# An encoder block on one core: query loads a unit earlier, gate stores on another queue, weight blocks a product later

## The chip, the cores and the metric

The kernel runs on one core of a Trainium2 chip. The metric is the device time of one execution in microseconds, as the median of several. The core's engines are TensorE (PE, with its weight loads shown as PEld), VectorE (DVE), ScalarE (ACT), GpSimd (POOL) and SyncE (SP). Each runs its own instruction stream in order. SP, ACT and POOL also issue DMA transfers; such an issue stands in the stream of its engine, behind what was written before it.

## The reference

One encoder layer over 1024 tokens of width 1024, all in float32:

```python
h = h + 0.5 * swiglu(rms_norm(h, ffn1_norm), ...)
u = rms_norm(h, mix_norm)
z = u @ w_in
q, k, v, s_in, gates = jnp.split(z, splits, axis=-1)
y_attn = neighbourhood_attention(q, k, v, na_rpb) @ w_attn_out
y_ssm = s5_branch(s_in, ...) @ w_ssm_out
g_attn, g_ssm = jnp.split(jax.nn.sigmoid(gates), 2, axis=-1)
h = h + (g_attn * y_attn + g_ssm * y_ssm) @ w_out
h = h + 0.5 * swiglu(rms_norm(h, ffn2_norm), ...)
h = h + (p @ w_ple_proj) * sigmoid(rms_norm(h, ple_norm) @ w_ple_gate)
return rms_norm(h, final_norm)
```

The attention has 8 heads of 64 over a grid of 16 rows by 64 columns, with a window of 8 by 16 and a learned bias per head. The state-space branch is a scan in both directions. The gates are two blocks of 1024 columns of `z`.

## The kernel before

Activations are kept transposed (features on the 128 partitions, tokens along the free axis, in two halves of 512). Each float32 operand is split into a high part, rounded to the type that TensorE takes (`split`, a cast on ACT at L159), and the rest (a subtraction on DVE at L160); a product of 128x128 by 128x512 is then three matmuls (`mm3`, L190 to L192). Large products use a recursive scheme with seven products for a two by two block product, in the order of `A7`, `ACC7` and `NEW7`.

The stages run in this order: first feed-forward block; the mixer; merging of the branches and output projection; second feed-forward block; the per-layer embedding; the final norm. The change is in the mixer alone.

In the mixer two streams of work are interleaved by hand on PE. The **main stream** goes through 84 products (`items`, 12 pairs of 7): the query and key projections (`qk`) and the gate projections (`g`). Each product is `s_run`: four `mm3`, and after each of them one `tick()`. A tick moves the **side stream** (`mixer_side`) on; `yield 3` in it means that its next piece comes three ticks later. The side stream does, one after another, the injection into the state-space scan, the attention, the outputs of the scan, and its gated linear unit.

The attention runs over 64 units: head `hd`, half of the rows `rb`, block of columns `cb` (0 to 3). In step `j` of its loop (L1346) the side stream loads the bias table (`load_tab`), asks for queries and keys (`load_q`, L1203; `load_k`, L1197), computes the scores of unit `j` (`attn_scores`, PE at L1228, bias and minimum on DVE at L1232, exponential and scaling on ACT at L1235 and L1237), transposes those of unit `j - 2` (`attn_turn`, PE at L1244), and multiplies unit `j - 4` by the values (`attn_values`, PE at L1255 and L1257). After the last column block of a half the output is put together on ACT and DVE (L1261, L1262) and stored (L1365). Two steps of the scan follow (`scan_steps`, POOL at L1154 to L1156), then `yield 3`. One set of queries, high and low part, serves the four column blocks of a half: `load_q` takes two buffers and issues four DMAs from DRAM through SP (L1208). It can run only when the projections of that head have been stored (`ready`).

The results of a product leave PSUM in `s_evac` (ACT copies at L1539, DVE additions at L1543). Gate results go to `s_out`, which appends their store to the list `later`; the list is emptied by `s_store` (L1546) in the next product, behind its third `mm3`. An entry of `later` names the engine that issues the transfer: ACT for values, keys and queries, POOL for gates (L1518). There are 32 gate stores of 256 KB, into `g_d`, read back after the mixer.

Weight blocks of 128x512 are loaded by `s_load` (L1499) through ACT's queue (L1506) and prepared by `s_prep`. `s_ahead(n + 1)` at the start of product `n` has asked for the loads up to product `n + LL` and the preparations up to `n + LP`, with `LL, LP = 5, 2` (L1567). Of the seven products of a pair, four load a block.

Query, value and weight tiles, the split weights, results on their way out and most other temporaries of the mixer share one pool of 24 buffers of 128x512 (`NM`, tag `m`). A tile that takes over a buffer waits until the last reader of the former one is done, a store included.

PE's order in the mixer is that of the program. The order of the other engines' instructions and DMA issues is set by the planner of the tool, which simulates the kernel with modelled times and picks what is ready by priority; evacuations are given a higher priority.

Of the kernel before, what the change touches and what calls it, by code (L numbers as in the profile page):

```python
# [21 lines left out]
NH = 8  # L22
# [19 lines left out]
def encoder_block(ctx, tc, I, out):  # L42
    nc = tc.nc
# [46 lines left out]
    def bank(name):  # L90
        return ps.tile([P, HT], F32, tag="ps", name=name)

    def dtile(name, shape):
        return dr.tile(list(shape), F32, name=name)
# [28 lines left out]
    g_d = dtile("g_d", [16, P, SEQ])  # L123
# [70 lines left out]
    def hsl(t):  # L194
        return slice(t * HT, (t + 1) * HT)
# [882 lines left out]
    def u_second():  # L1078
        yield 6
        un[1].stat()  # L1080
        yield 1
        for j in (0, 1, 2, 3, 4, 5, 6, 7):
            u_norm(j, 1)
            yield 1
        yield 3
        for k in range(4):
            G.tensor_tensor(h[4 + k][1], h[k][1], h[4 + k][1], ALU.add)
            s3 = tmp("s3")
            G.tensor_tensor(s3, h[k][0], h[k][1], ALU.subtract)
            nc.gpsimd.dma_start(s_d[k], s3)  # L1090
            yield 3
            u_put("s1", h[4 + k][1])
        for k in range(4):
            G.tensor_tensor(h[4 + k][1], h[4 + k][1], h[k][0], ALU.subtract)
            yield 2
            u_put("s2", h[4 + k][1])
        for k in range(4):
            G.tensor_tensor(h[4 + k][0], h[4 + k][0], h[4 + k][1], ALU.subtract)
            yield 2
            u_put("s4", h[4 + k][0])  # L1100
# [6 lines left out]
    def new_x():  # L1107
        xt = tl("h", 1, [P, 2 * XR], F32, "X")
        x0 = xt[:, 0:1]
        X.update(t=x0.tensor, o=x0.offset, p=x0.ap[0], v=xt.rearrange("p (r g n) -> p r g n", r=2, g=NPAIR))  # L1110
        for r in range(2):
            V.memset(X["v"][:, r, :, 0:1], 0.0)
            V.memset(X["v"][:, r, :, XP - 1:XP], 0.0)
# [6 lines left out]
    def inject_load(pr):  # L1120
        fm = [ta("fmi", [P, 256]) for _ in range(2)]
        for d in range(2):
            (nc.sync, nc.scalar)[d].dma_start(fm[d], f_d[pr, :, d * 256:(d + 1) * 256])
        return load_u(pr), fm

    def inject(pr, ut, fm):
        o = bank("inj")
        for g in range(2):
            for d in range(2):
                T.matmul(o[:, (2 * g + d) * NCH:(2 * g + d + 1) * NCH], lhsT=fm[d][:, g * P:(g + 1) * P],  # L1130
                         rhs=ut[:, g], start=True, stop=True)
        for g in range(2):
            for r in range(2):
                dst = X["v"][g * 64:(g + 1) * 64, r, pr, 1:1 + 2 * NCH]
                src = o[r * 64:(r + 1) * 64, g * 256:(g + 1) * 256]
                if g == r:
                    A.copy(dst, src)  # L1137
                else:
                    V.tensor_copy(dst, src)
# [10 lines left out]
    def scan_steps(n):  # L1150
        for c in range(scan["c"], min(scan["c"] + n, NCH)):
            x0, x1 = (xap(o, [[XP, 2 * NPAIR], [257 - 2 * o, 2]]) for o in (c, c + 1))
            both = xap(c, [[0, 2], [XP, 2 * NPAIR], [257 - 2 * c, 2]])
            G.tensor_tensor(sc, both, rho4, ALU.mult)  # L1154
            G.tensor_tensor(cross1, cross1, cross, ALU.add)  # L1155
            G.tensor_tensor(x1, sc[:, 0], x1, ALU.add)  # L1156
            scan["c"] = c + 1
# [52 lines left out]
    def load_v(hd, cb):  # L1210
        n = 4 * KNC[cb]
        hl = tmp("vhl", [P, 4, 2 * 64], F32R)
        nc.sync.dma_start(hl[0:n].rearrange("p g d -> p (g d)").bitcast(F32), vdr[hd, :, KC0[cb]:KC0[cb] + KNC[cb]])
        vld[hd, cb] = hl

    def load_tab(b, v):
        if b < 2 * NH:
            n = 12 * TN[v]
            tabs[b, v] = ta("tb")[:, 0:n]
            nc.sync.dma_start(tabs[b, v], I["tabs"][b, :, TOFF[v]:TOFF[v] + n])  # L1220
# [89 lines left out]
    def mixer_side():  # L1310
        yield from u_second()
        while 3 not in stored:
            yield 1
        yield 7
        new_x()
        ld = {}
        for pr in range(3):
            ld[pr] = inject_load(pr)
        yield 10
        for pr in range(NPAIR):  # L1320
            if pr + 3 < NPAIR:
                ld[pr + 3] = inject_load(pr + 3)
            inject(pr, *ld.pop(pr))
            yield 2
        while "v" not in stored:
            scan_steps(1)
            yield 1
        for cb in range(4):
            scan_steps(4)
            yield 4  # L1330
            load_v(0, cb)
        load_tab(0, 0)
        while 0 not in ready:
            scan_steps(1)
            yield 1
        units = [(hd, rb, cb) for hd in range(NH) for rb in range(2) for cb in range(4)]
        n = len(units)
        load_k(0)
        load_q(0, 0)
        for _ in range(6):  # L1340
            scan_steps(1)
            yield 2
        sms, pts, O = {}, {}, {}
        late.clear()
        lo, so = {}, {}
        for j in range(n + 5):  # L1346
            if j < n:
                hd, rb, cb = units[j]
                b = 2 * hd + rb
                load_tab(b + cb // 2, (1, 2, 0, 0)[cb]) if cb < 3 else None  # L1350
                if cb == 2 and rb == 0:
                    load_q(hd, 1)
                if cb == 2 and rb == 1 and hd + 1 < NH:
                    while hd + 1 not in ready:
                        yield 1
                    load_q(hd + 1, 0)
                if rb == 0 and cb == 2 and hd + 1 in ready:
                    load_k(hd + 1)
                if rb == 1 and cb == 2 and hd + 1 < NH and hd + 1 not in khl:
                    load_k(hd + 1)  # L1360
                sms[j] = attn_scores(hd, rb, cb)
            if 0 <= j - 2 < n:
                pts[j - 2] = attn_turn(units[j - 2][2], sms.pop(j - 2))
            while late:
                nc.scalar.dma_start(*late.pop())  # L1365
            if 0 <= j - 4 < n:
                hd, rb, cb = units[j - 4]
                if cb == 0:
                    O[hd, rb] = bank("O")
                attn_values(hd, rb, cb, O[hd, rb], *pts.pop(j - 4))  # L1370
                if rb == 1 and hd + 1 < NH:
                    load_v(hd + 1, cb)
            scan_steps(2)
            if j >= n:
                if j - n < 3:
                    lo[j - n] = ssm_load(j - n)
            yield 3
        scan_steps(NCH)
        for p in range(NPAIR + 1):
            if 3 <= p + 3 < NPAIR:  # L1380
                lo[p + 3] = ssm_load(p + 3)
            if p < NPAIR:
                so[p] = ssm_out(p, *lo.pop(p))
            if p > 0:
                so.pop(p - 1)()
            yield 1 + p % 2
        yield 3
        glu_load(0)
        raws = [glu_raw(0), glu_raw(1)]
        yield 11  # L1390
        glu_act(0)
        glu_load(1)
        yield 2
        glu_act(1)
        for t in range(2):
            yield from glu_half(t, raws)
# [99 lines left out]
    later = []  # L1496
# [14 lines left out]
    def s_out(n, c, t, second, src):  # L1511
        kind, m = pairs[n]
        if kind == "g":
            if c == "21":
                z, src = tmp("z21"), src
                A.copy(z, src)
                src = z
            later.append((nc.gpsimd, g_d[2 * m + second, :, hsl(t)], src))  # L1518
            return
        hi, lo = tmp("qkh", dt=F32R), tmp("qkl", dt=F32R)  # L1520
        if second:
            A.activation(hi, src, AF.Copy, scale=0.125)
            V.scalar_tensor_tensor(lo, src, 0.125, hi.bitcast(F32), ALU.mult, ALU.subtract)
        else:
            def view(x):
                return x.rearrange("p (b r c) -> p r b c", b=4, r=8)
            sv = src.rearrange("p (r b c) -> p r b c", r=8, b=4)
            A.copy(view(hi), sv)
            V.tensor_tensor(view(lo), sv, view(hi).bitcast(F32), ALU.subtract)
        for i, x in enumerate((hi, lo)):  # L1530
            later.append((nc.scalar, (k_d if second else q_d)[m, i, :, hsl(t)], x.bitcast(F32)))
# [32 lines left out]
        with tc.high_priority(offset=PRI):  # L1564
            s_evac(n, i)

    LL, LP = 5, 2  # L1567
    done_ = {"l": 0, "p": 0}

    def s_ahead(n):  # L1570
# [137 lines left out]
    for m0 in range(0, NK, 2):  # L1708
# [15 lines left out]
        if m0 in (2, 4):  # L1724
            out_load(2 if m0 == 2 else 0)
            with tc.issue_after(mark["gt"]):
                for j in range(NK):
                    t = m0 // 2 - 1
# [229 lines left out]
```

## Time and profile before

| | us |
|---|---|
| median of 3 runs | 2112.91 (2112.85 to 2114.22) |
| the profiled execution | 2113.88 |
| its span, from the first to the last instruction | 2112.1 |
| DVE busy | 1468.4 |
| ACT busy | 1011.0 |
| POOL busy | 480.2 |

The profile page gives the busy time of each engine, the granted clock of TensorE over the span, and the groups of instructions that cost most. Further views of the trace give busy times by stretch, who waited for whom, and the instructions in order of time. In a timeline a row has the start, the duration, engine, line, operation, output and inputs; brackets give the idle time of the engine just before it and what ended that. In a list of waits the numbers are the total, the count and the longest. An engine name with a q (SPq, ACTq) is its DMA queue.

### The profile page before, as it was taken

To read this page: it belongs to the slowest core of one execution; us is meant where nothing else is said; L and a number is where in the kernel's file an instruction comes from. 1 tells how busy PE (TensorE), PEld (TensorE's weight loads), DVE (VectorE), ACT (ScalarE), POOL (GpSimd) and SP (SyncE) were. 2 spreads that over 40 slices of the span, in tenths; PEclk is the share of its full clock that TensorE was granted. 3 is DMA by queue.
4 is the path that set the end of the run, shared out by engine and by line. 5 is a ranking of instruction groups with operands and counts; after the bars stand their busy time and mean duration, and the time that the engine had idled before them with its cause. 6 is when DMAs were issued, how large, how long until landed. Compare 5 with 4: busy or idle time off the path is not lost.

```text
span 2112.1 us, 28243 instructions
## 1 busy us (share of the span) xinstructions
PE 2060.9 (98%) x9518; PEld 1685.9 (80%) x9518; DVE 1468.4 (70%) x2478; ACT 1011.0 (48%) x1878; POOL 480.2 (23%) x720
## 2 busy tenths in 40 slices
PE   9999999999999998898999999999999999999998
PEld 3788888888888887777888788788888888888887
DVE  7897776667967847555655669896565665785855
ACT  6434333344445535656655546553333334445544
POOL 0037565540000518888031002000000000000000
PEclk9999999999999999999999999999999999999999
DMA  3434444485543557566675776143323338533302
GB/s 131 142 118 152 129 131 128 139 284 156 185 120 107 149 180 238 171 197 192 192 243 185 231 264 164 65 154 102 123 80 121 99 100 293 170 105 95 115 26 80
DMA packets 212464, 319.75 MB, mean 151 GB/s; under 512 B 37856, under 2 KB 81504, under 8 KB 212320
## 3 DMA queue, kind: packets, MB, share of 16 engines
q1 hardware_dynamic: 173840, 258.14, 38.9%
q10 hardware_dynamic: 31760, 44.07, 6.3%
q0 software_dynamic: 6720, 15.75, 2.6%
q8 instruction: 75, 1.23, 0.2%
q14 instruction: 69, 0.57, 0.1%
HBM read 224.01 MB, written 93.85 MB: 150 GB/s over the span
## 4 chain that ended last, share of the span: by engine, by line
PE 80%; POOL 7%; DVE 5%; DMA 3%; ACT 2%; issue 2%; SPq 0%; ACTq 0%; DVEq 0%; POOLq 0%
PE dx L190 4%; PE dx L191 4%; PE dx L192 4%; PE gx L190 3%; PE ux L190 3%; PE ux L192 3%; PE gx L192 3%; PE gx L191 3%; PE ux L191 3%; POOL sc L1154 3%; PE dy L192 2%; PE dy L190 2%; PE dy L191 2%; POOL X L1156 2%; POOL sc L1155 2%
## 5 line engine op out<-in xcount | busy, mean ns | idle before, releaser
L159 ACT CAST wh<-hbuf 128x512 fp32r<-128x512 f32 x280 | 173.0, 622 | 389.2 <-PE gx L191 84.3
L160 DVE TENSOR_TENSOR wl<-hbuf,wh 128x512 fp32r<-128x512 f32 x280 | 215.4, 772 | 121.7 <-ACT wh L159 119.7
L159 ACT CAST wh<-wblk 128x512 fp32r<-128x512 f32 x190 | 117.9, 622 | 188.7 <-PE dx L191 82.4
L160 DVE TENSOR_TENSOR wl<-wblk,wh 128x512 fp32r<-128x512 f32 x190 | 130.6, 690 | 49.8 <-ACT wh L159 40.2
L190 PE MATMUL dx<-ah,wh 128*128 128x512 f32 x416 | 163.5, 393 | 0.4 <-DVE hbuf L694 0.3
L192 PE MATMUL dx<-ah,wl 128*128 128x512 f32 x416 | 161.9, 389 | 0.0
L191 PE MATMUL dx<-al,wh 128*128 128x512 f32 x416 | 161.9, 389 | 0.0
L160 DVE TENSOR_TENSOR al<-araw,ah 128x512 fp32r<-128x512 f32 x154 | 106.5, 696 | 49.6 <-PE dx L191 21.1
L190 PE MATMUL gx<-xh,wh 128*128 128x512 f32 x320 | 125.0, 391 | 1.3 <-DVE c L581 1.2
L190 PE MATMUL ux<-xh,wh 128*128 128x512 f32 x320 | 125.0, 390 | 0.0
L191 PE MATMUL gx<-xl,wh 128*128 128x512 f32 x320 | 124.5, 389 | 0.0
L192 PE MATMUL ux<-xh,wl 128*128 128x512 f32 x320 | 124.5, 389 | 0.0
L192 PE MATMUL gx<-xh,wl 128*128 128x512 f32 x320 | 124.5, 389 | 0.0
L191 PE MATMUL ux<-xl,wh 128*128 128x512 f32 x320 | 124.5, 389 | 0.0
L159 ACT CAST ah<-araw 128x512 fp32r<-128x512 f32 x154 | 94.9, 619 | 44.5 <-PE dx L191 14.2
L160 DVE TENSOR_TENSOR wl<-blk,wh 128x512 fp32r<-128x512 f32 x84 | 61.4, 733 | 49.6 <-ACT wh L159 47.2
L190 PEld LDWEIGHTS dx<-ah,wh 128*128 128x128 f32 x416 | 78.1, 188 | 18.6 <-DVE hbuf L694 1.2
L191 PEld LDWEIGHTS dx<-al,wh 128*128 128x128 f32 x416 | 78.1, 188 | 16.8 <-issue 0.7
L428 DVE TENSOR_TENSOR hbuf<-hbuf 128x512 f32<-128x512 f32 x120 | 89.7, 749 | 2.1
L192 PEld LDWEIGHTS dx<-ah,wl 128*128 128x128 f32 x416 | 78.1, 188 | 16.3
L1154 POOL TENSOR_TENSOR sc<-X,rho 128x128 f32<-128x128 f32 x128 | 75.5, 590 | 59.4 <-ACT X L1137 49.6
L190 PE MATMUL px<-xh,wh 128*128 128x512 f32 x192 | 80.6, 420 | 6.1 <-ACT z L1539 4.7
(399 smaller groups left out, 5775.6 us busy)
## 6 DMA issues: line engine op xcount, KB each, us to landing
araw<-a_d SPq DMA_DIRECT2D x154, 256.0 KB
a_d<-c SPq DMA_DIRECT2D x148, 256.0 KB
wblk<-in_wd SPq DMA_DIRECT2D x88, 256.0 KB
hbuf<-in_wg SPq DMA_DIRECT2D x40, 512.0 KB
hbuf<-in_wu SPq DMA_DIRECT2D x40, 512.0 KB
blk<-in_win ACTq DMA_DIRECT2D x48, 256.0 KB
hbuf<-in_xT SPq DMA_DIRECT2D x32, 256.0 KB
h_d<-hbuf ACTq DMA_DIRECT2D x32, 256.0 KB
```

Of the source, the lines that this page charges most:

```text
L159: A.copy(hi, src)
L160: return eng.tensor_tensor(lo, src, hi.bitcast(F32), ALU.subtract)
L190: T.matmul(o, lhsT=wh, rhs=xh, start=first, stop=False, skip_group_check=more)
L191: T.matmul(o, lhsT=wh, rhs=xl, start=False, stop=False, skip_group_check=more)
L192: T.matmul(o, lhsT=wl, rhs=xh, start=False, stop=last, skip_group_check=more)
L428: V.tensor_tensor(b11, (b12, b22, None, None, b21)[i - 2], b11, ALU.subtract)
L1154: G.tensor_tensor(sc, both, rho4, ALU.mult)
L1155: G.tensor_tensor(cross1, cross1, cross, ALU.add)
L1156: G.tensor_tensor(x1, sc[:, 0], x1, ALU.add)
```

## The change

Queries are asked for at column block 1 instead of 2, so three units ahead of their first use instead of two. Gate stores are issued by ACT instead of POOL. Weight blocks are asked for four products ahead instead of five.

```diff
@@ mixer_side
                 load_tab(b + cb // 2, (1, 2, 0, 0)[cb]) if cb < 3 else None
-                if cb == 2 and rb == 0:
+                if cb == 1 and rb == 0:
                     load_q(hd, 1)
-                if cb == 2 and rb == 1 and hd + 1 < NH:
+                if cb == 1 and rb == 1 and hd + 1 < NH:
                     while hd + 1 not in ready:
                         yield 1
                     load_q(hd + 1, 0)
@@ s_out
-            later.append((nc.gpsimd, g_d[2 * m + second, :, hsl(t)], src))
+            later.append((nc.scalar, g_d[2 * m + second, :, hsl(t)], src))
             return
@@
-    LL, LP = 5, 2
+    LL, LP = 4, 2
```

## The prediction

> **What bounds the kernel now.** I read the page's head first, then the busy time by stretches, then the waits of TensorE one by one, and for each long one the timeline of the engine that ended it.
>
> ```profile
> span 2112.1 us, 28243 instructions
> PE 2060.9 (98%) x9518; PEld 1685.9 (80%) x9518; DVE 1468.4 (70%) x2478; ACT 1011.0 (48%) x1878; POOL 480.2 (23%) x720
> 780.00:1065.00 285.00, 257.60 (x1424) 218.24 (x1423) 173.89 (x413) 170.76 (x387) 197.66 (x400) 0.95 0.64 191
> 1065.00:1200.00 135.00, 128.79 (x673) 107.97 (x671) 71.81 (x126) 75.68 (x143) 28.07 (x48) 1.00 0.70 219
> ```
>
> TensorE (PE) is busy 98% of the span, so the change can win only where PE is idle or slow. The last two rows (stretch, its length, busy time of PE, PEld, DVE, ACT, POOL, then the granted clock) cover the mixer's side work. From 780 to 1065, where attention runs, PE is idle 285 - 257.6 = 27.4 us and its clock is 0.95: another 0.05 x 285 = 14 us are lost. From 1065 to 1200 it is idle 6.2 us at full clock. All that the change can win lies in the first row. Its parts, by narrower stretches:
>
> ```profile
> 865.00:885.00 20.00, 14.30 (x71) 11.83 (x70) 8.94 (x24) 9.29 (x22) 17.72 (x37) 0.83 0.40 132
> 955.00:975.00 20.00, 13.96 (x75) 11.78 (x75) 9.77 (x24) 9.99 (x24) 16.94 (x40) 0.83 0.59 182
> 895.00:905.00 10.00, 7.53 (x36) 6.01 (x35) 4.93 (x13) 5.26 (x13) 8.43 (x21) 0.83 0.65 211
> 913.00:930.00 17.00, 14.50 (x78) 12.14 (x77) 8.33 (x21) 10.22 (x24) 14.57 (x32) 0.90 0.75 202
> 985.00:1010.00 25.00, 22.08 (x125) 18.73 (x124) 14.13 (x37) 15.53 (x38) 16.56 (x37) 0.93 0.62 191
> 785.00:805.00 20.00, 16.82 (x68) 13.54 (x67) 11.07 (x19) 9.15 (x20) 17.27 (x35) 0.91 0.69 212
> ```
>
> Each row loses its idle time plus (1 - clock) x length: 5.7 + 3.4 = 9.1; 6.0 + 3.4 = 9.4; 2.5 + 1.7 = 4.2; 2.5 + 1.7 = 4.2; 2.9 + 1.7 = 4.6; 3.2 + 1.8 = 5.0 us. A stall is followed by a stretch at lower clock, so it costs more than its idle time. [...]
>
> The first two losses begin at a gate store:
>
> ```profile
> 859.94 0.69 DVE L1543 TENSOR_TENSOR z<-pz,z 128x512 f32<-128x512 f32 x1 [0.35 <-PE pz L192]
> 868.39 0.58 POOL L1549 DMA_DIRECT2D g_d<-z  x1
> 870.80 0.68 DVE L1262 TENSOR_TENSOR ot<-O,ol 64x512 f32<-64x512 f32 x1 [9.20 <-DMA g_d<-z]
> 872.02 0.54 ACT L1237 ACTIVATE sm<-sm,stat 128x288 f32<-128x288 f32 x1 [9.36 <-DVE stat L1236]
> 872.61 0.87 PE L1244 MATMUL pt<-ident,sm 128*96 128x128 f32 x3 [5.47 <-ACT sm L1237]
> ```
>
> The gate block z is ready at 860.6, but POOL, busy with the scan, issues its store at 868.4. DVE's next output (ot) has been given the buffer of a z, waits 9.2 us for the store to land, and holds everything behind it: ACT's softmax 9.4 us, PE 5.5 us. So some 9.2 - 5.5 = 3.7 us of such a hold are covered.
>
> ```profile
> 945.09 0.59 ACT L1516 COPY z<-px 128x512 f32<-128x512 f32 x1
> 954.12 0.56 POOL L1549 DMA_DIRECT2D g_d<-z  x1
> SPq L1213 <- DMA g_d<-z: 6.8, 1, 6.8
> SPq L1208 <- DMA g_d<-z: 5.8, 1, 5.8
> 965.02 0.58 PE L1228 MATMUL s<-khl,ql 128*128 128x288 f32 x1 [3.35 <-DMA ql<-q_d]
> ```
>
> Here z is ready at 945.7 and stored at 954.1; SP's loads, in one queue, wait for its buffer (6.8, then 5.8 us), and PE waits for the queries. The other three losses are query loads as well:
>
> ```profile
> 983.18 0.34 PE L1228 MATMUL s<-khl,qh 128*128 128x384 f32 x1
> 986.44 0.34 PE L1228 MATMUL s<-khl,qh 128*128 128x384 f32 x1
> 988.05 1.14 SPq L1208 DMA_DIRECT2D qh<-q_d  x2
> 989.28 1.18 SPq L1208 DMA_DIRECT2D ql<-q_d  x2
> 995.39 0.37 PE L1228 MATMUL s<-khl,qh 128*128 128x288 f32 x1 [2.35 <-DMA qh<-q_d]
> 996.33 0.37 PE L1228 MATMUL s<-khl,ql 128*128 128x288 f32 x1 [0.57 <-DMA ql<-q_d]
> 900.61 0.37 PE L1228 MATMUL s<-khl,ql 128*128 128x288 f32 x1 [2.15 <-DMA ql<-q_d]
> 918.10 0.37 PE L1228 MATMUL s<-khl,ql 128*128 128x288 f32 x1 [0.61 <-DMA ql<-q_d]
> 1025.29 0.37 PE L1228 MATMUL s<-khl,qh 128*128 128x288 f32 x1 [1.49 <-DMA qh<-q_d]
> ```
>
> The loads are asked for with the unit scored at 986.44 (cb 2), two units ahead of their use, and the last has landed by 996.3: 9.9 us. PE came for them at 995.39 - 2.35 = 993.0, 6.6 us after the asking, and waited 2.4 + 0.6 us. The loads leave SP 1.6 us after they are asked, so the lead sets their time, not a buffer.
>
> **The change part by part.**
>
> *Queries three units ahead.* Four DMAs per block move from cb 2 to cb 1, past SP's bias-table and value loads of one unit; their number stays. The lead grows by one unit, 986.44 - 983.18 = 3.3 us, and asking at 983.2 plus 9.9 gives 993.1, just when PE came. In the rows above, every wait for queries but that at 965 is at most 2.9 us, so 3.3 us cover it. Worth 4.2 + 4.2 + 4.6, with the 1.5 at 1025 and some 0.5 in smaller ones, gives 14.5. Where a head's queries are not yet stored the loop holds one unit earlier; PE then does projections, so nothing is added. I take 13, since the lead is only just enough.
>
> ```profile
> DVE sm L1232 <- DMA tb<-in_tabs: 2.5, 2, 1.4
> ```
>
> The table and value loads now stand behind four query issues, 2.4 us of SP (988.05 to 990.46). Values are used four units later and tables two, and DVE waits for tables only 2.5 us in all; were that cover gone, a table 2.4 us late would still lie under DVE's 3.7.
>
> *Gate stores through ACT's queue.* 32 issues leave POOL and join ACT behind the instruction that makes z, or DVE's. POOL's freed time is worth nothing: in the list of PE's waits from 780 to 1065 below (the four last rows: total, times, longest) none is on the scan. What goes is the late store: 9.1 + 9.4 = 18.5 (for the second the longer lead alone would cover 3.3 of the 6.0). Next late is then the buffer's former cover, a store issued within a product of z.
>
> ```profile
> L1549 ACTq DMA_DIRECT2D k_d<-qkh x8: 332/333/461, 804.6 to 974.8; - x8
> L1549 ACTq DMA_DIRECT2D v_d<-vs x16: 366/404/1057, 755.7 to 792.2; - x16
> 794.35 0.62 ACT L159 CAST wh<-blk 128x512 fp32r<-128x512 f32 x1 [3.03 <-DMA v_d<-vs]
> 796.03 0.80 PE L190 MATMUL px<-xh,wh 128*128 128x512 f32 x1 [3.18 <-ACT z L1539]
> PE s L1228 <- DMA qh<-q_d: 8.7, 5, 2.7
> PE s L1228 <- DMA ql<-q_d: 8.4, 7, 3.4
> PE pt L1244 <- ACT sm L1237: 5.5, 1, 5.5
> PE px L190 <- ACT z L1539: 4.7, 3, 3.2
> ```
>
> The added wait: ACT is in order, so a store that waits for z holds the softmax steps (L1235, L1237), the casts (L159) and evacuations (L1539) behind it, and PE waits for these. An issue is 0.33 us, so 32 are 10.7 us on an engine that is busy 171 of 285: beside PE's work. No row shows a gate store held there. The lower end is nothing, the key and query stores already going that way with no PE wait on them in that list. The upper end comes from the nearest row: of 16 value stores on ACT's queue one hold of 3.0 us reached PE, the 5.0 us of 785 to 805. One in 16 of 32 is 2 x 5.0 = 10 us, and I take that end, since ACT is fuller here than the lower end needs.
>
> *Weight blocks four products ahead* (LL 5 to 4). 48 loads stay on ACT and go one product later, 4/3 of a unit or 4.3 us; each buffer is held that much less.
>
> ```profile
> DVE blk L428 <- DMA blk<-in_win: 13.1, 8, 3.8
> ```
>
> DVE waits for a late block eight times, at most 3.8 us, which the 3.7 us of cover just hide. Upper end: the two or three longest get 4.3 longer, some 4 us each on PE, 12 in all. Lower end: the stall at 796, where a block load held up behind the value stores keeps ACT, goes: -5. I take 0, as the planner that orders DVE places the subtraction by when it believes the block is there. On buffers the two size changes nearly cancel: 16 x 2 query tiles held 3.3 us longer (106), 48 blocks 4.3 us shorter (206).
>
> **Sum.** -13 - 18.5 + 10 + 0 = -21.5 us. The profiled execution took 2113.88 us, 1.8 more than its span, against a median of 2112.91: 2113.9 - 21.5 = 2092.4, so **2092 us**. PE is the bound behind 1065, so what is won there stays won.
>
> **The rivals.** *SP doesn't send earlier.* The order of SP's queue is the planner's; if it places the queries where they were, the query part is 0 and of the stall at 955 to 975, 3.3 us with 1.7 of clock stay: -18.5 + 5 + 10 = -3.5, so 2110. For it: the SP queue's waits for buffers above; against it: at 988 the loads left 1.6 us after being asked.
>
> *ACT is held.* Gate stores on ACT wait for z, the softmax waits behind them, and PE behind that, at 5.0 us each. The point of decision is (13 + 18.5) / 5.0 = 6.3 stores of 32: at nine it is -31.5 + 45 = +13.5, so 2127, slower than before. For it: the hold at 794. Against it: the key stores, 0.33 us each, pass ACT in the same stretch and none of the list's waits follows from them.
>
> *The store lands as late from any queue.* Then only the query part is left: 2113.9 - 13 = 2101. The row against it: 7.8 us pass between z and the issue, 2.4 from issue to DVE's start. [...]
>
> **How the numbers follow.** A measurement of this kernel can tell about 0.2% (4.2 us) from no change. The forecast (2081 to 2105) 0.62, the store as late (2101) 0.09, SP not earlier (2110) 0.13, ACT held at about break-even (2109 to 2117) 0.03, ACT held beyond it 0.13. Faster is 0.62 + 0.09 = 0.71, same 0.16, slower 0.13. The low end is both parts whole with no price on ACT, 2113.9 - 14.5 - 18.5 = 2080.9, and half of the 5 us at 796: 2078. The high end takes in SP not earlier and break-even: 2114. Left out is the held ACT.
>
> **What would show it.** Right: from 780 to 1065 PE idle at 10 to 15 us in place of 27.4, clock at 0.98 or more, no wait of DVE or SP for g_d, query waits under 5 us in all (17 now). Wrong: PE waiting for ACT's sm or z right behind an ACT issue of g_d; query loads still leaving SP 6 to 7 us ahead of their scores; DVE L428 waiting far over 13 us for blocks.

## The result, and the profile after

| | before | after |
|---|---|---|
| median, us | 2113.56 (2112.85 to 2114.79) | 2094.23 (2089.91 to 2097.08) |
| runs | 4 | 4 |
| ratio, with 95% interval | | 0.9907 (0.9891 to 0.9923) |
| the profiled execution, us | 2113.88 | 2089.91 |

The kernel is 0.93% faster, 19.3 us by the medians. The forecast was 2092, in a range from 2078 to 2114. The profiled execution after is the fastest of its four, 4.3 us under the median, so what is read from its trace is a little too good. First the head of the page of the changed kernel, with the last line from the chain that ended last:

```profile
span 2088.1 us, 28214 instructions
PE 2053.6 (98%) x9518; PEld 1680.4 (80%) x9518; DVE 1468.1 (70%) x2478; ACT 1010.5 (48%) x1878; POOL 468.4 (22%) x688
...
PE 86%; DVE 6%; DMA 5%; ACT 2%; issue 1%; ACTq 0%; SPq 0%; DVEq 0%
```

DVE and ACT do the same work as before. POOL has 32 instructions fewer (720 before), as many as there are gate stores. POOL was 7% of the chain before; it isn't in the chain now. The busy times by stretch say where the time came from: first the kernel before from 780 to 1200 (the whole part with side work), then the changed kernel. The columns are those of the prediction.

```profile
780.00:1200.00 420.00, 386.39 (x2095) 326.21 (x2094) 245.70 (x538) 246.44 (x529) 225.73 (x448) 0.97 0.66 200
```

```profile
780.00:1065.00 285.00, 273.35 (x1585) 233.23 (x1584) 188.96 (x443) 184.40 (x419) 198.96 (x392) 0.99 0.70 213
780.00:1200.00 420.00, 402.42 (x2197) 339.95 (x2196) 265.06 (x566) 261.52 (x553) 213.28 (x415) 0.99 0.71 219
```

From 780 to 1200 PE was idle 420 - 386.4 = 33.6 us and is idle 420 - 402.4 = 17.6 us now: 16.0 less. The clock rose from 0.97 to 0.99 of 420 us, which is another 12.6 - 4.2 = 8.4 us. Together they make 24.4, and the spans differ by 24.0. So the gain lies in this stretch, some two thirds of it idle time and one third clock (the clock is read to two digits, so its part is uncertain by some 3 us). In the stretch on which the prediction rested, 780 to 1065, the idle time fell from 27.4 to 11.65 us. The list of waits of the changed kernel in that stretch (total, count, longest; first rows of PE, then one of DVE and one of SP's queue):

```profile
PE pt L1244 <- ACT sm L1237: 5.6, 5, 2.6
PE px L190 <- ACT z L1539: 2.6, 2, 2.2
...
PE s L1228 <- DMA ql<-q_d: 0.2, 1, 0.2
...
DVE blk L428 <- DMA blk<-in_win: 22.6, 10, 4.8
SPq L1208 <- DMA g_d<-z: 7.3, 4, 3.8
```

And two rows of the kernel before, for the same queue and stretch, which the prediction did not show:

```profile
DVE blk L428 <- DMA blk<-in_win: 11.7, 6, 3.8
...
SPq L1208 <- DMA g_d<-z: 25.6, 3, 14.7
```

PE's 17 us of waits for queries are 0.2 us. DVE no longer waits for a gate store at all, and the wait of SP's query loads for the buffer of one fell from 25.6 to 7.3. DVE's wait for weight blocks doubled (the prediction's 13.1 is that of the whole execution, of which 11.7 lie in this stretch). Last, the timeline of the changed kernel at a gate store and at a set of queries:

```profile
861.58 0.67 DVE L1543 TENSOR_TENSOR z<-pz,z 128x512 f32<-128x512 f32 x1
862.28 0.33 ACTq L1549 DMA_DIRECT2D g_d<-z  x1
...
963.80 0.34 PE L1228 MATMUL s<-khl,qh 128*128 128x384 f32 x1
966.29 2.04 SPq L1208 DMA_DIRECT2D qh<-q_d  x2
968.43 1.17 SPq L1208 DMA_DIRECT2D ql<-q_d  x2
973.93 0.29 PE L1228 MATMUL s<-khl,qh 128*128 128x288 f32 x1
```

The gate block is ready at 861.58 + 0.67 = 862.25 and its store is issued 0.03 us later, where the prediction read 7.8 us for POOL. That 7.8 is the least it can have been. In the kernel before, an older gate block was ready at 852.04 + 0.69 = 852.73:

```profile
852.04 0.69 DVE L1543 TENSOR_TENSOR z<-py,z 128x512 f32<-128x512 f32 x1
```

The store at 868.39 is the first gate store of that execution, so this block had then been waiting 15.7 us. The trace doesn't name which block a store takes. It does show that not all 32 stores were late: POOL stood idle for its block before the eight stores from 1004.94 to 1052.75. The eight stores from 868 to 954 are those that stood behind the scan. The queries are asked for with the scores at 963.80 and used at 973.93 without a wait: a lead of 10.1 us in place of 6.6.

### The profile page after: what moved, and what is told of

Read it like the earlier page. It is cut to its first block, busy times and chain, and to the rows that moved or that the text cites. A ratio compares the mean times of both kernels' runs of the same rounds, so it can differ in the third digit from the quotient of the medians.

```text
span 2088.1 us, 28214 instructions
## 1 busy us (share of the span) xinstructions
PE 2053.6 (98%) x9518; PEld 1680.4 (80%) x9518; DVE 1468.1 (70%) x2478; ACT 1010.5 (48%) x1878; POOL 468.4 (22%) x688
## 4 chain that ended last, share of the span: by engine, by line
PE 86%; DVE 6%; DMA 5%; ACT 2%; issue 1%; ACTq 0%; SPq 0%; DVEq 0%
PE dx L190 4%; PE dx L191 4%; PE dx L192 4%; PE gx L190 3%; PE ux L190 3%; PE ux L192 3%; PE gx L191 3%; PE gx L192 3%; PE ux L191 3%; PE dy L191 2%; PE dy L192 2%; PE dy L190 2%; DMA blk<-in_win 2%; PE uy L190 2%; PE gy L190 2%; PE uy L192 2%
## 5 line engine op out<-in xcount | busy, mean ns | idle before, releaser
L160 DVE TENSOR_TENSOR wl<-hbuf,wh 128x512 fp32r<-128x512 f32 x280 | 217.4, 779 | 122.9 <-ACT wh L159 120.8
L160 DVE TENSOR_TENSOR wl<-wblk,wh 128x512 fp32r<-128x512 f32 x190 | 130.8, 691 | 50.7 <-ACT wh L159 43.2
L160 DVE TENSOR_TENSOR al<-araw,ah 128x512 fp32r<-128x512 f32 x154 | 106.6, 696 | 50.7 <-PE dx L191 18.3
L1154 POOL TENSOR_TENSOR sc<-X,rho 128x128 f32<-128x128 f32 x128 | 82.4, 644 | 59.4 <-ACT X L1137 49.4
L160 DVE TENSOR_TENSOR wl<-blk,wh 128x512 fp32r<-128x512 f32 x84 | 60.9, 727 | 43.4 <-ACT wh L159 42.9
```

The source lines that it names most:

```text
L160: return eng.tensor_tensor(lo, src, hi.bitcast(F32), ALU.subtract)
```

## The experiments

Each kernel was timed against the kernel before on the same chip, and the ratio and its interval are to that. Ratios are turned into microseconds with 2113.

### Each part alone

The three parts can be taken apart without touching one another. In the first kernel only the queries are asked for earlier:

```diff
-                if cb == 2 and rb == 0:
+                if cb == 1 and rb == 0:
...
-                if cb == 2 and rb == 1 and hd + 1 < NH:
+                if cb == 1 and rb == 1 and hd + 1 < NH:
```

> Only the queries are asked for three units ahead. Separate terms: the query waits of PE (17.1 us before) fall to the 6 us that hang on a late gate store, and with their stretches at lower clock some 13 us go, so about 2100 (ratio 0.994). The rival that the planner does not send the loads earlier gives no change (ratio 1.000). The rival that the parts help only together, because they share 24 buffers, gives less than 5 us (ratio above 0.998). The wait of DVE for a gate store to free its buffer (9.2 us) stays in each of them.

Measured: 2108.44 us, ratio 0.9978 (0.9966 to 0.9990), a gain of 4.6 us where 13 were forecast. PE's waits in this kernel, from 780 to 1065:

```profile
PE pt L1244 <- ACT sm L1237: 18.1, 7, 7.5
PE px L190 <- ACT z L1539: 5.8, 3, 3.2
PE py L190 <- ACT z L1539: 0.8, 1, 0.8
```

There is no row for queries: all 17 us of those waits are gone, so the longer lead does what it says. But PE waits 18.1 us for ACT's softmax, 5.5 before, and its idle time in the stretch fell only from 27.4 to 285 - 259.9 = 25.1 us. The timeline of the same kernel shows why:

```profile
864.14 0.68 DVE L1543 TENSOR_TENSOR z<-pz,z 128x512 f32<-128x512 f32 x1
873.05 0.58 POOL L1549 DMA_DIRECT2D g_d<-z  x1
875.15 0.68 DVE L1262 TENSOR_TENSOR ot<-O,ol 64x512 f32<-64x512 f32 x1 [9.49 <-DMA g_d<-z]
876.96 0.87 PE L1244 MATMUL pt<-ident,sm 128*96 128x128 f32 x3 [7.55 <-ACT sm L1237]
...
1013.31 0.62 ACT L159 CAST wh<-blk 128x512 fp32r<-128x512 f32 x1 [8.66 <-DMA g_d<-z]
1014.42 0.87 PE L1244 MATMUL pt<-ident,sm 128*96 128x128 f32 x3 [4.60 <-ACT sm L1237]
```

The last of three gate blocks is ready at 864.8, and a store behind the scan leaves POOL at 873.05. Whoever has been given the buffer of a late store waits: DVE's output here, and at 1004 to 1013 a cast on ACT. The hold on DVE was there before as well (9.2 us). The one on ACT was not: the stores of that group, prompt in the kernel before, stand behind the scan here. And one of the stores from 937 to 953, a group that had made PE wait for queries before, now holds a cast on ACT for 3.6 us, and PE for 2.2. What follows: the query stall was real, but while gate stores are late, most of what it costs moves and doesn't go.

The second kernel moves only the gate stores:

```diff
-            later.append((nc.gpsimd, g_d[2 * m + second, :, hsl(t)], src))
+            later.append((nc.scalar, g_d[2 * m + second, :, hsl(t)], src))
```

> Only the gate stores go through ACT's queue. Separate terms: the stall of PE at 867 to 872 and most of the one at 958 to 965 go (18.5 us, of which some 5 stay because the queries there are still asked for late), ACT's holds take back up to 10: between -4 and -14 us, 2100 to 2110 (ratio 0.993 to 0.998). The rival that a store lands as late from any queue gives no change and a wait of DVE for g_d as long as before. The rival that ACT is held gives a ratio above 1.002 and waits of PE for ACT's sm right behind an ACT issue of g_d.

Measured: 2102.07 us, 0.9943 (0.9924 to 0.9962), a gain of 12.0 us. PE's waits in this kernel, 780 to 1065:

```profile
PE s L1228 <- DMA ql<-q_d: 6.7, 8, 1.5
PE px L190 <- ACT z L1539: 3.9, 2, 3.3
PE s L1228 <- DMA qh<-q_d: 3.2, 3, 1.9
PE pt L1244 <- ACT sm L1237: 1.2, 1, 1.2
```

The query waits fell from 17.1 to 9.9 us, none over 1.9, though the lead is the old one, two units. Of the 7.2 us that went, 6.0 are the waits at 961 and 965 (2.7 and 3.4 us), where SP's loads had waited for the buffer of a late store. The prediction had booked these on the gate part, rightly. The other query waits are nearly all still there, 9.9 of 11.1 us. No wait in this list follows from a gate store on ACT.

The third kernel changes only the weight blocks:

```diff
-    LL, LP = 5, 2
+    LL, LP = 4, 2
```

> Only the weight blocks are asked for one product later. The prediction's term is 0: ratio 1.000 within 0.2%. Its lower end is -5 us, if the stall of PE at 793 to 796 goes; its upper end is +12 us, if DVE waits for blocks (13.1 us before at L428) grow to some 25 us and reach PE. A theory of buffers gives a gain here: with one block fewer in the 24 buffers, query and value loads wait less.

Measured: 2110.66 us, 0.9984 (0.9974 to 0.9994), a gain of 3.4 us by the ratio. The interval lies just clear of 1, but the gain is under the 4.2 us (0.2%) that the prediction took as the least that can be told from no change. PE's waits for queries in this kernel, 780 to 1065, and DVE's for blocks:

```profile
PE s L1228 <- DMA ql<-q_d: 6.6, 6, 2.2
PE s L1228 <- DMA qh<-q_d: 4.4, 3, 3.1
...
DVE blk L428 <- DMA blk<-in_win: 18.1, 8, 4.2
```

The query waits are 11.0 us in place of 17.1, and the waits for blocks 18.1 in place of 11.7. That is what one would see if blocks asked for later land later and leave their buffers to the queries for longer. That the buffers are the reason is not shown: with the gate stores on ACT, the same step leaves the query waits no shorter (9.9 us with five products, 12.0 with four, below).

### Two parts, the third left out

The queries with the gates (weight blocks at five):

> Queries three units ahead and gate stores on ACT's queue, weight blocks five products ahead as before. If the weight blocks are worth nothing, this is the changed kernel: 2094 within 3 us (ratio 0.991). If the waits of DVE for late blocks, 22.6 us at L428 in the changed kernel against 13.1 before, reach PE, this one is faster than the changed kernel by 3 to 8 us. If the freed buffers are what lets the query loads go early, it is slower than the changed kernel by 5 us or more and PE waits for queries again.

Measured: 2096.80 us, 0.9919 (0.9902 to 0.9935). This is the changed kernel within the intervals, and PE's query waits are 1.2 us, so the freed buffers aren't what lets the query loads go early. Against the gate stores alone the query waits fell from 9.9 to 1.2 us, but PE's waits for the softmax and for evacuations on ACT rose from 5.1 to 12.1: here too most of the wait came back elsewhere.

The gates with the blocks (queries at column block 2):

> Gate stores on ACT's queue and weight blocks one product later, queries two units ahead as before. If the three parts add up (queries alone -4.6, gates alone -11, blocks alone -2.4 us), about 2100 (ratio 0.994), and PE's waits for queries, 9.9 us with the gate stores alone, stay near 10. If the freed buffers let the query loads go earlier, the query waits fall well below 10 us and the time comes near the changed kernel's 2094.

Measured: 2102.49 us, 0.9947 (0.9935 to 0.9960). Its interval does not touch that of the changed kernel (0.9891 to 0.9923). PE's query waits are 12.0 us. The query part is therefore worth 0.40%, 8.5 us, when both others are there.

The queries with the blocks, gate stores back on POOL:

```diff
-            later.append((nc.scalar, g_d[2 * m + second, :, hsl(t)], src))
+            later.append((nc.gpsimd, g_d[2 * m + second, :, hsl(t)], src))
```

> The changed kernel with the gate stores back on POOL: queries three units ahead and weight blocks four products ahead alone. If the parts add up (-4.6 and -2.4), about 2106 (ratio 0.997). In the kernel with the queries alone PE no longer waited for queries, but 18.1 us for ACT's sm, the longest 7.5 behind a store of g_d; that should be here again, 12 us or more, with DVE or ACT waiting 8 us or more for one gate store. If it were the buffers that count, two query tiles more held and one block less, PE's idle time would be near that of the changed kernel (11.7 us from 780 to 1065).

Measured: 2105.32 us, 0.9969 (0.9956 to 0.9981), again clear of the changed kernel by 0.62%, 13.1 us. The waits of this kernel, from 780 to 1065:

```profile
PE pt L1244 <- ACT sm L1237: 13.4, 5, 7.3
...
PE s L1228 <- DMA ql<-q_d: 0.6, 1, 0.6
...
ACT wh L159 <- DMA g_d<-z: 13.3, 2, 6.9
ACT z L1516 <- DMA g_d<-z: 8.3, 1, 8.3
```

It is the picture of the queries alone: 0.6 us of waits for queries is left, and the late gate stores hold three instructions of ACT for 21.6 us in all, and PE behind the softmax.

### What the gate stores cost on ACT

The prediction charged 10 us for ACT's issues. Two kernels ask for that price. In the first, the stores leave through SP, for which the page lists no busy time:

```diff
-            later.append((nc.scalar, g_d[2 * m + second, :, hsl(t)], src))
+            later.append((nc.sync, g_d[2 * m + second, :, hsl(t)], src))
```

> The changed kernel with its 32 gate stores issued by SP instead of ACT. If only POOL's late issue was the cost, another prompt queue does as well: ratio against the kernel before 0.990 to 0.993. If a store on ACT costs some 10 us of holds, as the prediction took, this one is up to 10 us faster than the changed kernel (ratio near 0.986). The rival: a store that waits for z in SP's queue holds the query and value loads behind it, PE waits for queries again, and the ratio is above 0.994.

Measured: 2094.06 us, 0.9909 (0.9894 to 0.9924), the changed kernel's ratio within 0.02%. PE's waits for ACT's softmax are 7.4 us in seven (5.6 in five on ACT), its waits for queries 1.1 us. Taking 32 issues from ACT gains nothing that can be measured. By itself this doesn't bound their price on ACT, since SP pays something too: its queue stands 21.1 us behind gate blocks that aren't ready, and DVE's waits for tables are 9.0 us in place of 2.9. The trace of the changed kernel answers more directly. From 780 to 1065 it has 20 gate stores on ACT. Only one of them has ACT standing idle for more than 1.3 us up to the instruction behind it, leaving aside waits for PE's results. It is the store at 922.78:

```profile
923.16 0.54 ACT L1237 ACTIVATE sm<-sm,stat 128x288 f32<-128x288 f32 x1 [2.15 <-DMA vhl<-v_d]
```

PE didn't wait there. None of its nine waits of 0.3 us or more ends within 5 us behind a gate store. So in this execution no wait of PE hangs on a gate store on ACT, where the prediction took 10 us for them.

In the second, ACT stores each gate block twice, the second time into a buffer in DRAM that nothing reads:

```diff
             later.append((nc.scalar, g_d[2 * m + second, :, hsl(t)], src))
+            later.append((nc.scalar, g2_d[2 * m + second, :, hsl(t)], src))
```

> The changed kernel, with every gate block stored twice by ACT, the second time to a buffer in DRAM that nothing reads: 32 issues of 0.33 us and 8 MB more. If a gate store on ACT's queue costs PE 0.3 us each, as the prediction's 10 us for 32 has it, this one is 10 us slower than the changed kernel (about 2104, ratio 0.996). If ACT's issues lie beside PE's work, it is within 3 us of the changed kernel (ratio 0.990 to 0.992).

Measured: 2105.02 us, 0.9954 (0.9941 to 0.9967), about 10 us (0.47%) slower than the changed kernel. From 780 to 1065 PE is idle 18.5 us against 11.65, and one stall is most of the difference (lines are shifted: L1238, L1245 and L1551 are L1237, L1244 and L1549 of the others):

```profile
870.30 0.33 ACTq L1551 DMA_DIRECT2D g_d<-z  x1
870.68 0.61 ACT L1238 ACTIVATE sm<-sm,stat 128x384 f32<-128x384 f32 x1 [5.47 <-DMA vhl<-v_d]
871.35 0.90 PE L1245 MATMUL pt<-ident,sm 128*128 128x128 f32 x3 [6.35 <-ACT sm L1238]
```

A gate store stands in front of the softmax in ACT's stream, ACT is idle up to it, and PE waits 6.35 us. The clock from 860 to 880 is 0.74 (1.00 in the changed kernel; PE's products of 128x512 take 0.63 us from 873.4 to 876.4, and 0.39 again from 878.6), another 5.2 us: together 11.5, as much as the whole difference of 10 us. This is the hold that the prediction feared, on one of 64 stores. The row names a landing of values, not the gate block, as what ended the wait; why the store waited for that stays open. The run gives no price for an issue by itself, since the second stores move 8 MB more (32 times 256 KB) and hold each buffer longer too. It shows how a store on ACT can cost some 11 us at once, when it falls in front of a softmax that PE needs.

### Where the weight blocks' price begins

The blocks are asked for three products ahead:

```diff
-    LL, LP = 4, 2
+    LL, LP = 3, 2
```

> The changed kernel with weight blocks asked for three products ahead instead of four. DVE's waits for blocks at L428 were 13.1 us with five, 22.6 with four (queries and gates changed as well) and 18.1 with four alone. If asking later costs through these waits, they grow beyond 25 us, PE waits for DVE's casts or ACT's sm, and this is 4 to 12 us slower than the changed kernel (ratio 0.993 to 0.997). If fewer blocks in the buffers is a gain, it is 1 to 3 us faster (ratio 0.989 to 0.990).

Measured: 2113.95 us, 1.0002 (0.9991 to 1.0013): the whole gain of the change is lost by one step more, 20 us where 4 to 12 were expected. The waits of DVE and ACT in this kernel, 780 to 1065:

```profile
DVE blk L428 <- DMA blk<-in_win: 33.0, 14, 5.1
...
ACT wh L159 <- DMA blk<-in_win: 19.0, 11, 5.2
```

The same row of the kernel with queries and gates, where the blocks are five ahead:

```profile
DVE blk L428 <- DMA blk<-in_win: 19.8, 10, 5.3
```

With queries and gates as in the change, DVE's waits for blocks at five, four and three products are 19.8, 22.6 and 33.0 us. Most of their growth over the 11.7 of before is there at five already, so it comes with the other two parts. From five to four the time does not suffer (0.9919 and 0.9907); at three, ACT waits 19.0 us for blocks as well (2.3 in the changed kernel). PE is idle 19.0 us in this stretch, 7.3 more than in the changed kernel, and 135 - 123.1 = 11.9 us from 1065 to 1200, 6.0 more. With the lower clock (0.98 from 780 to 1200 against 0.99, some 4 us) that is most of the 20 us; the rest was not followed up.

### Does the longer hold of the query buffers cost

The longer lead keeps query tiles in the pool for longer. With two buffers fewer:

```diff
-NM = 24
+NM = 22
```

> The changed kernel with 22 buffers of 128x512 in place of 24 in the mixer's shared pool. If the waits of SP for buffers are covered by the leads now, it is within 4 us of the changed kernel (ratio 0.990 to 0.993). If the shared buffers still set when loads can start, query waits of PE come back (0.2 us now) and it is 8 us or more slower (ratio above 0.995).

Measured: 2097.35 us, 0.9933 (0.9918 to 0.9949), 0.26% (5.5 us) above the changed kernel, between the two cases expected, with intervals that overlap. SP's wait for buffers of gate stores doubles, from 7.3 to 14.3 us, but PE waits for queries 0.2 us as before. So the pool doesn't set the time through the query loads. Whether two buffers fewer cost something elsewhere is not told apart from noise, and more than 24 were not tried.

### What is left, and two attempts at it

The longest attention stall that is left in the changed kernel, in its timeline:

```profile
941.54 0.85 DVE L428 TENSOR_TENSOR blk<-blk 128x512 f32<-128x512 f32 x1 [4.65 <-DMA blk<-in_win]
...
942.96 0.61 ACT L1237 ACTIVATE sm<-sm,stat 128x384 f32<-128x384 f32 x1 [6.01 <-DVE stat L1236]
...
943.62 0.55 PE L1244 MATMUL pt<-ident,sm 128*128 128x128 f32 x3 [2.62 <-ACT sm L1237]
```

A weight block that comes late holds DVE for 4.65 us, DVE holds ACT's softmax, and PE waits 2.62: some 2 us of such a hold are covered. To widen that cover, the transposes run three units behind the scores and the values five:

```diff
-            if 0 <= j - 2 < n:
-                pts[j - 2] = attn_turn(units[j - 2][2], sms.pop(j - 2))
+            if 0 <= j - 3 < n:
+                pts[j - 3] = attn_turn(units[j - 3][2], sms.pop(j - 3))
```

The loop gets one step more, and the values take `j - 5` for `j - 4` in the same way.

> The changed kernel with the transposes three units behind the scores instead of two, and the products with the values five instead of four: the softmax on DVE and ACT gets one unit, 3.3 us, more before PE asks for it. If the softmax is what comes late next now that queries and gate stores don't hold it, PE's waits for ACT's sm (5.6 us) go, and it is 4 to 8 us faster than the changed kernel (ratio 0.987 to 0.989). If PE then waits somewhere else for the same DVE and ACT (casts of weights, evacuations), it is within 3 us of the changed kernel. A slower one would mean that the tiles held longer (scores, values) delay the loads of tables and values.

Measured: 2091.71 us, 0.9909 (0.9893 to 0.9925). PE's waits in this kernel, 780 to 1065:

```profile
PE s L1228 <- DMA ql<-q_d: 4.4, 5, 1.2
PE px L190 <- ACT z L1539: 3.5, 3, 2.2
PE py L190 <- ACT z L1539: 3.4, 1, 3.4
```

The waits for the softmax are gone, and waits for queries and for evacuations on ACT took their place. The gain is nil.

The other stall left is that at 795, 2.15 us, which the prediction put down to the value stores ahead of a block load on ACT's queue (its lower end for the blocks, -5). Here the value stores leave through SP:

```diff
-                later.append((nc.scalar, vds[...
+                later.append((nc.sync, vds[...
```

> The changed kernel with the 16 value stores issued by SP instead of ACT. The stall of PE before 796 (2.2 us and 3.4 us at half clock) followed ACT's burst of value stores from 787 to 793; if issues in a burst are what holds ACT there, it goes and this is 2 to 5 us faster than the changed kernel (ratio 0.988 to 0.990). If the value casts of ACT and DVE themselves hold it, no change (within 2 us).

Measured: 2094.17 us, 0.9919 (0.9905 to 0.9932): no gain. In its timeline the stall is still there, with another cause:

```profile
798.29 0.62 ACT L159 CAST xh<-s 128x512 fp32r<-128x512 f32 x1 [3.45 <-DMA s<-s_d]
...
799.45 0.50 PE L190 MATMUL py<-xh,wh 128*128 128x512 f32 x1 [2.43 <-ACT z L1539]
```

ACT now waits for an activation block in place of a weight block. None of the runs beats the changed kernel clear of its interval.

## Why the prediction was right, and where it was not

The time came out 2 us above the forecast, but two terms were off in opposite directions.

| us, from differences of ratios x 2113 | forecast | alone | beside one other | beside both |
|---|---|---|---|---|
| queries | -13 | -4.6 | gates -5.1, blocks -3.2 | -8.5 |
| gates | -18.5 + 10 = -8.5 | -12.0 | queries -12.5, blocks -7.8 | -13.1 |
| blocks | 0 | -3.4 | queries -1.9, gates +0.8 | -2.5 |

The half-widths of the intervals are 0.0010 to 0.0019, so a difference of two ratios is uncertain by some 4 us. The three alone add up to 0.22 + 0.57 + 0.16 = 0.95%, and the whole is 0.93%.

**The bound.** Right. All of the gain lies where the prediction looked, in idle time and clock between 780 and 1200, and nothing was given back behind it.

**Queries, -13.** The mechanism was right: the loads leave SP earlier, PE's waits for them went from 17.1 us to none in the queries alone, 3.3 us more of lead covered what was short. Mis-sized was "4.2 + 4.2 + 4.6": each stretch was booked as if it went whole with its query wait. In the kernel with the queries alone most of the idle time came back as waits for the softmax, 18.1 us in place of 5.5. The query term is 3 to 8.5 us. The prediction asked "what is late next" only for the gate stores. For the queries alone the next late thing was the gate stores themselves; with prompt gate stores it was the softmax and the evacuations (12.1 us in place of 5.1).

**Gates, -18.5.** The mechanism was right: z to issue fell from 7.8 us or more to 0.03, DVE's wait for a store is gone. Of SP's rows the expectation "no wait of DVE or SP for g_d" fails: 7.3 us are left on L1208, in pieces of at most 3.8; PE's query waits are 0.2 us all the same. One rival is left in part. The change also takes the stores off POOL's own queue, on which they needed 2.3 to 6.9 us from issue to landing (median 4.4). For ACT's queue the trace has no such time, so how much of the gain is a faster landing, and not the earlier issue, is not told apart.

**ACT's price, +10.** This was the step that failed in size. In the changed kernel's trace no gate store on ACT holds PE, and with the stores on SP the time is the same (0.9909 against 0.9907). The hold itself is real: with every block stored twice one store of 64 cost some 11 us. So it was right to name it, and at 10 us it was priced as if two of 32 would fall badly; none did. The row it was priced from was no sure sign: the hold at 794 ends with the landing of a value store, and with the value stores on SP a stall as long stayed at that place. The net term of the gates is -12 to -13 us in three of the four settings, -7.8 beside the blocks alone. That is still less than the -18.5 of the term without a price: as with the queries, it seems that not all of a stretch's loss goes with the wait that is seen in it. The excess of the gates, 4 us, and what the blocks brought balance most of the queries' shortfall. So the forecast was nearer than its terms, and that it came within 2 us is luck in part.

**Blocks, 0.** Within its bounds and near the value taken. The price that it named, DVE waiting longer for blocks, is real, but small at this step, 19.8 to 22.6 us; it breaks through one product further. The gain that it named at 796 is real too, and a fifth of its 5 us: the stall there is 3.2 to 3.3 us in the kernel before and in the three others with five products, and 2.1 to 2.2 in the changed kernel and the three with one or two of its parts that ask four ahead. Against it, in these four PE waits 2.2 to 2.3 us at 814 to 826 for a subtraction on DVE (L160) that none of the others waits for. The prediction's buffer sum doesn't "nearly cancel": 106 against 206 leaves 100 us of one buffer, of 24 x 285 = 6840 in the stretch. Whether the blocks bring the 2.5 us that the table has beside both stays open, since the intervals of the two kernels overlap.

**The rivals.** *SP doesn't send earlier* is refuted by the queries alone, which leave no wait for queries. *ACT is held* did not happen in the changed kernel, by its trace; the equal time through SP agrees, within the 4 us that a difference is uncertain by. It did happen once where the blocks are stored twice. *The store lands as late from any queue* is refuted by the kernel with the gates undone: 13 us. With ACT and with SP as issuers the time is one (0.9907 and 0.9909), with POOL it is another (0.9969): what was saved there was not only the time of an issue, 0.58 us on POOL and 0.33 on ACT, but 7.8 us or more in line behind the scan.

**What would show it.** Idle from 780 to 1065 of 10 to 15 us: 11.65. Clock at 0.98 or more: 0.99. Query waits under 5 us: 0.2. Of the wrong signs, query loads no longer leave 6 to 7 us ahead; DVE's waits for blocks did go far over 13 us, and the gain came all the same, so that sign was badly chosen.

## What to carry to other kernels

Where many short-lived tiles share one pool, a late store is a stall that picks its victim by who takes the buffer next; repairing the victim moves the stall (with the queries alone, PE's waits for queries went from 17.1 us to none and those for the softmax from 5.5 to 18.1), and issuing the store from an engine that isn't busy ahead of it removes it (DVE's wait of 9.2 us is gone), as long as no store there falls in front of work that is waited for (6.35 us of PE, with each block stored twice). So book a gain to the cause, and ask of each wait that is taken away which late thing the engine meets next. Shortening a lead looks free until its cover ends (ratio 0.9919 at five products, 0.9907 at four, 1.0002 at three): try one step further before believing that it is.

## What the runs showed of the hardware

In the changed kernel a stall's cost in clock was not set by its length alone: a stall of 2.15 us was followed by a lower clock, one of 2.6 us was not. Stretches of the changed kernel, columns as before:

```profile
790.00:795.00 5.00, 2.85 (x13) 2.07 (x12) 1.70 (x3) 2.29 (x5) 4.24 (x10) 1.00 1.06 322
795.00:800.00 5.00, 5.00 (x16) 3.92 (x16) 5.00 (x7) 3.46 (x8) 4.53 (x7) 0.66 0.60 198
...
940.00:945.00 5.00, 2.38 (x18) 1.94 (x17) 2.25 (x6) 2.04 (x5) 4.25 (x10) 1.00 0.42 121
945.00:950.00 5.00, 4.51 (x26) 3.60 (x25) 3.37 (x11) 4.66 (x13) 4.22 (x11) 1.00 0.57 186
```

After the 2.15 us of idle that end at 794.75 the clock is 0.66 over 5 us, which is 1.7 us lost: it is 0.50 in each half microsecond from 796.0 to 799.0, and 0.91 and 0.67 in those just before and behind. After 5 - 2.38 = 2.6 us of idle that end at 943.62 it stays at 1.00 and nothing is lost. No run here moved a stall in time and left the rest as it was, so what sets the two apart is not shown. Run to run, the changed kernel's four times lie between 2089.91 and 2097.08 us, 0.34% apart.
